# One buffer for an MLP chunk's activations and their sums, one copy and one subtraction to split it, and dependent sums spread over turns

## The chip, the cores and the metric

The kernel runs on one core of a Trainium2 chip. The metric is the time of one execution on the device in microseconds (us). Engines in the profile: PE is TensorE (PEld its weight loads), DVE is VectorE, ACT is ScalarE, POOL is GpSimd, SP is the engine whose queue issues most DMAs.

## The reference

One layer of a decoder trunk on 256 tokens of width 1024, in float32: a gated sum of a convolution branch and a sparse attention branch, a cross attention, and an MLP with squared relu, then a last RMSNorm. The change is in the MLP, and in a few buffers of the attention's index scores:

```python
def reference(x, mem, ...):
    ...
        h = h + (g_conv * y_conv + g_attn * y_attn) @ w_mix_out[l]
        h = h + _cross_attention(...)
        hf = _rmsnorm(h, norm_ffn_g[l]) @ w_ff1[l]            # (256, 1024) @ (1024, 4096)
        h = h + jnp.square(jax.nn.relu(hf)) @ w_ff2[l]        # (256, 4096) @ (4096, 1024)
    return _rmsnorm(h, norm_final_g)
```

## The kernel before

**Products in three terms.** The matmuls run in a rounded float32 format (`F32R`). To keep float32 accuracy both operands are split into a high part (a copy into `F32R`, on ScalarE) and a low part (the operand minus its high part, on VectorE), and a product is high*high + high*low + low*high (`mm3`). So each weight and each activation costs one ScalarE copy and one VectorE subtraction.

**The stream of weights.** All weights come in chunks of 1 MB (`raw`, 128 x 2048 elements) in the order of `STREAM`, through three buffers. `load()` issues the next one on SP's queue. It is called where the last low part of an earlier chunk is issued, so a load waits on the chip until that buffer's last reader, a VectorE subtraction, is done. Every chunk becomes a few jobs in `high_jobs` (normally two halves). `split_high()` takes the first job and issues its ScalarE copy; `split_low()` issues the VectorE subtraction of the job before it, and calls `prepare()` of the job that is second in the list; `split_ahead()` does one `split_low` and one `split_high`, and is called once per tile of matmuls. At most five halves are split ahead.

**The MLP.** The hidden width of 4096 is cut into 16 chunks of 256 features. `("f1", c)` is the slice of the first weight and `("f2", c)` that of the second. `first(x, side, wide)` computes 128 of the 256 features for all tokens into a PSUM bank `ps_f`, taken from the two `mm` banks. With `wide` the three terms go into two halves of a bank that have to be merged (a ScalarE copy and a VectorE sum). The loop over `c` does `first(c+2, 0)`, the first half of chunk c's second product, `first(c+2, 1)`, and its second half. So an activation is made two chunks ahead of its use.

**Chunks with seven products.** For the chunks in `SEVEN` the second product is a 2 x 2 block product of activation blocks (feature half k, token block r, each 128 x 128) and weight blocks (128 x 512). It is computed with seven block products instead of eight, which needs sums of blocks on both sides. The weight's sums (`seven`) are `outer` (two sums in one instruction) and `inner` (two instructions, of which the second reads the first's result); its jobs are `left`, `last`, `outer`, `inner`. The activation's sums (`fn`) are one instruction of two blocks and two instructions that depend on each other. Chunks 0, 1 and 5 use six products, chunks 13 to 15 four.

**The activation of a chunk** is a generator, `activation`, one for each 128 features (`ct`): relu out of PSUM and square on ScalarE into `ft`, the sums `fn` on VectorE, then for each group of blocks a ScalarE copy into `sh` and a VectorE subtraction into `sl` (both parts of `fs`). For a chunk with seven products these are three copies (1, 2 and 4 blocks) and three subtractions.

**Turns.** Generators are in `chains`. `tick()` runs each of them up to its next `yield`; it is called after each tile. `finish(chain)` calls `tick()` until that chain has ended, and `Hidden.done()` does so for both chains of a chunk. A turn thus advances all chains: besides the activations, `turn_rows` (sixteen small DMAs into `h_rm`, one in each turn) and `ff_scale`, which sums the squares of h (`sums_ff`) for the MLP's RMSNorm and, three turns after its last square, sends `ps_ff` matmuls to TensorE. The order in which the instructions are issued in this program is the order in which each engine runs them.

Of the kernel before, what the change touches and what calls it, by code (L numbers as in the profile page):

```python
# [114 lines left out]
def block_kernel(ctx, tc, x, xt, mem, memt, wst, wki, vecs, convw, gout, out):  # L115
# [21 lines left out]
    def w2(name, dt=F32, shape=(P, 512)):  # L137
        return work.tile(list(shape), dt, tag="w2", bufs=8, name=name)

    def bank(tag, bufs, name):  # L140
        return psum.tile([P, 512], F32, tag=tag, bufs=bufs, name=name)

# [58 lines left out]

    class Stage:

        def __init__(self, key, high, before=None, slot=True):
            self.key, self.high, self.before, self.slot = key, high, before, slot
            if not slot:
                elsewhere.add(key)

        def prepare(self):
            if self.before:  # L210
                self.before()
                self.before = None

    def seven(key, c, raw):

        b = raw.rearrange("p (k h n) -> p k h n", k=2, h=2)
        flat = raw.rearrange("p (j n) -> p j n", j=4)
        sums = []

        def outer():  # L220
            sums.append(t8(f"sums{c}", F32, (P, 4, 512)))
            dve.tensor_tensor(out=sums[0][:, 0:2, :], in0=flat[:, 0:4:3, :],
                              in1=flat[:, 1:2, :].to_broadcast([P, 2, 512]), op=ALU.add)

        def inner():
            t = sums[0]
            dve.tensor_tensor(out=t[:, 2, :], in0=t[:, 1, :], in1=flat[:, 0, :], op=ALU.add)
            dve.tensor_tensor(out=t[:, 3, :], in0=t[:, 2, :], in1=flat[:, 2, :], op=ALU.add)

        def stage(name, src_of, n, before=None):  # L230
            def high():
                src = src_of()
                if before:
                    both = t8(f"{name}{c}", F32R, (P, 2, 2, 512))
                    hi, lo = both[:, 0], both[:, 1]
                else:
                    hi = highs.tile([P, N_CHUNK // 2], F32R, tag="hi", name=f"hi{c}{name}")
                    lo = lows.tile([P, N_CHUNK // 2], F32R, tag="lo", name=f"lo{c}{name}")
                    hi, lo = (w[:, : n * 512].rearrange("p (j n) -> p j n", j=n) for w in (hi, lo))
                act(hi, src, AF.Copy)  # L240

                def low():
                    dve.tensor_tensor(out=lo, in0=src, in1=hi.bitcast(F32), op=ALU.subtract)
                    prepared[(*key, name)] = (hi, lo)
                    if name == "inner":
                        load()

                low_jobs.append(low)

            return Stage((*key, name), high, before, not before)  # L250

        return [stage("left", lambda: b[:, :, 0, :], 2), stage("last", lambda: flat[:, 3:4, :], 1),
                stage("outer", lambda: sums[0][:, 0:2, :], 2, outer), stage("inner", lambda: sums[0][:, 2:4, :], 2, inner)]

    def high(key, c, raw, ns, q, last):
        n = ns.stop - ns.start
# [16 lines left out]
    def split_high():  # L273
        if high_jobs and (not high_jobs[0].slot or nsplit[0] - nused[0] < HALVES - held[0]):
            job = high_jobs.pop(0)
            nsplit[0] += job.slot
            job.prepare()
            job.high()

    def split_low():  # L280
        if low_jobs:
            low_jobs.pop(0)()
        if len(high_jobs) > 1:
            high_jobs[1].prepare()

    nsplit, nused, held = [0], [0], [1]

# [149 lines left out]
    load()  # L437
    zero = w2("zero")
    nc.vector.memset(zero, 0.0)
    zero_r = cst.tile([P, 512], F32R, name="zero_r")  # L440
    nc.vector.tensor_copy(zero_r, zero)
    ident = cst.tile([P, P], F32, name="ident")
    make_identity(nc, ident)
# [3 lines left out]
    nc.gpsimd.memset(onesd, 1.0 / D)  # L447
    table = cst.tile([P, 1], F32, name="table")
    nc.gpsimd.memset(table, 0.0)
    ki2 = cst.tile([P, S], F32, name="ki2")  # L450

    nc.scalar.activation(half, half, AF.Sigmoid, bias=0.0, scale=0.0)
    nc.gpsimd.memset(half, -0.5)
# [185 lines left out]
    tick()  # L639
    wi = cst.tile([P, 2, 8], F32, name="wi")  # L640

    bias = [cst.tile([P, P * (qb + 1)], F32, name=f"bias{qb}") for qb in range(2)]

    def causal(t, qb, value):
        tail = t[:, qb * P :]
# [19 lines left out]
    def index_scores():  # L665
# [3 lines left out]
        dve.tensor_copy(wi, ps[:, :16].rearrange("p (r h) -> p r h", r=2))  # L669
        for qb in range(2):  # L670
            nk = P * (qb + 1)
            score = cst.tile([P, nk], F32, name=f"score{qb}")
            per = 512 // nk
            for g in range(4 // per):
                banks = [ps_acc(f"ps_idx{qb}{g}{j}").rearrange("p (a n) -> p a n", a=per) for j in range(2)]
                for a in range(per):
                    for j in range(2):
                        rows = slice(64 * j, 64 * j + 64)
                        pe.matmul(banks[j][:, a, :], qi_t[rows, per * g + a, qb * P : qb * P + P], ki2[rows, :nk],
                                  start=True, stop=True)  # L680
                for j in range(2):
                    rl = w2(f"rl{qb}{g}{j}", F32, (P, per, nk))
                    act(rl, banks[j], AF.Relu)
                    yield
                    for a in range(per):
                        h = 2 * (per * g + a) + j
                        if h == 0:
                            dve.tensor_scalar(score, rl[:, a, :], wi[:, qb, 0:1], None, ALU.mult)
                        else:
                            dve.scalar_tensor_tensor(out=score, in0=rl[:, a, :], scalar=wi[:, qb, h : h + 1], in1=score,  # L690
                                                     op0=ALU.mult, op1=ALU.add)
            causal(score, qb, NEG_FILL)
            yield
            fill.insert(0, choose(qb, score))
# [466 lines left out]
    start(turn_rows())  # L1161
    start(ff_scale())

    def activation(c, ct, ps, t, sh, sl):
        if ps.shape[1] == S:
            act(t[:, ct, :], ps, AF.Relu)  # L1166
        else:
            yield from merge(t[:, ct, :], ps)
            yield
            act(t[:, ct, :], t[:, ct, :], AF.Relu)  # L1170
        act(t[:, ct, :], t[:, ct, :], AF.Square)
        yield
        flat = t.rearrange("p k (r n) -> p (k r) n", r=2)
        if c not in SEVEN:
            cs = [(slice(2 * ct, 2 * ct + 2), flat[:, 2 * ct : 2 * ct + 2, :])]
        else:
            cs = [(slice(1, 3), flat[:, 2:4, :]) if ct else (slice(0, 1), flat[:, 0:1, :])]
        if ct and c < JOINED:
            n = w2(f"fn{c}", F32, (P, 4, P))
            if c in SEVEN:  # L1180
                dve.tensor_tensor(out=n[:, 0:2, :], in0=flat[:, 1:2, :].to_broadcast([P, 2, P]), in1=flat[:, 0:4:3, :],
                                  op=ALU.subtract)
                dve.tensor_tensor(out=n[:, 2, :], in0=flat[:, 0, :], in1=n[:, 1, :], op=ALU.subtract)
                dve.tensor_tensor(out=n[:, 3, :], in0=flat[:, 2, :], in1=n[:, 2, :], op=ALU.subtract)
                cs.append((slice(3, 7), n))
            else:
                dve.tensor_tensor(out=n[:, 0:2, :], in0=flat[:, 0:4:2, :], in1=flat[:, 1:4:2, :], op=ALU.subtract)
                cs.append((slice(4, 6), n[:, 0:2, :]))
        for js, src in cs:
            act(sh[:, js, :], src, AF.Copy)  # L1190
        yield
        for js, src in cs:
            dve.tensor_tensor(out=sl[:, js, :], in0=src, in1=sh[:, js, :].bitcast(F32), op=ALU.subtract)

    class Hidden:

        def __init__(self, c):
            self.c, self.jobs = c, []
            parts = t8(f"fs{c}", F32R, (P, 2, 7, P))
            self.hi, self.lo = parts[:, 0], parts[:, 1]  # L1200
            self.t = w2(f"ft{c}", F32, (P, 2, S))

        def after(self, ct, ps):
            self.jobs.append(start(activation(self.c, ct % 2, ps, self.t, self.hi, self.lo)))
# [2 lines left out]
            return self.hi[:, j, :], self.lo[:, j, :]  # L1207

        def row(self, k, rb):
            return self.of(2 * k + rb)  # L1210

        def done(self):
            for job in self.jobs:
# [31 lines left out]
            seventh(x, name)  # L1245
            tick()

    TERMS = {"left": (("1", 0), ("2", 1)), "last": (("3", 6),), "outer": (("5", 4), ("7", 3)), "inner": (("6", 5), ("4", 2))}

    def seventh(x, name):  # L1250
        w = weights("f2", x.c, name, None)
# [18 lines left out]
        return ap.rearrange("p (k f) -> p k f", f=P)  # L1270

    def last_residual(rb, ps, lo, hi):
        h = h_rm[:, lo // P : hi // P, rb, :]
        ps = by_tiles(ps)
        dve.scalar_tensor_tensor(out=h, in0=ps, scalar=r2[0][:, rb : rb + 1], in1=h, op0=ALU.mult, op1=ALU.add)

    def last_squares(rb, n, lo, hi):

        h = h_rm[:, lo // P : hi // P, rb, :]
        junk = w2(f"junk_o{rb}{n}")  # L1280
        act(by_tiles(junk[:, : hi - lo]), h, AF.Square, scale=1.0 / 32, accum_out=ss[:, rb, n : n + 1])
        if hi == D:
# [4 lines left out]
    def last_norm(rb, n):  # L1287
# [4 lines left out]
        for n, (lo, hi) in enumerate(((0, 352), (352, 704), (704, D))):  # L1292
# [2 lines left out]
                dve.tensor_scalar(cols, cols, scale, None, ALU.mult)  # L1295
            else:
                act(cols, cols, AF.Copy, scale=scale)
            (nc.scalar if n == 2 else nc.sync).dma_start(out[rb, :, lo:hi], cols)

    def add_to(rb, hf, ps, scales):  # L1300
        h = h_rm[:, 4 * hf : 4 * hf + 4, rb, :]
        dve.scalar_tensor_tensor(out=h, in0=by_tiles(ps), scalar=scales[:, rb : rb + 1], in1=h, op0=ALU.mult, op1=ALU.add)

    for c in range(JOINED):
        hidden.append(Hidden(c + 2))
        x, later = hidden[c], hidden[c + 2]
        wide = c not in SEVEN and c != 5
        first(later, 0, wide)
        x.done()
        if c in (0, 1, JOINED - 1):  # L1310
            split_ahead()
        half_of(x, 0)
# [130 lines left out]
```

## Time and profile before

| | |
|---|---|
| median of 3 runs | 505.08 us (504.98 to 505.32) |
| the profiled execution | 505.25 us, span 503.5 us |
| granted TensorE clock, mean | 0.998 |
| PE busy | 493.6 us, 98% of the span |
| DVE busy | 459.9 us, 91% |
| ACT busy | 349.1 us, 69% |
| POOL busy | 31.6 us, 6% |
| HBM read | 91.16 MB, 183 GB/s over the span |

The page gives shares over the whole span. A row of the timeline is: start in us from the span's start, duration in us, engine, line, operation, output <- inputs, partitions x elements, count, and in brackets the idle time of the engine before it and what ended that. Rows with a count above 1 are several instructions of one kind in sequence. A row of the chain that ended last has start, duration, engine and tile. Numbers of `ps_p`, `hi` and `lo` tiles are left out, but `hi58left` is the high part of the `left` job of `raw` number 58, which is `("f2", 2)`; 60, 62 and 66 are chunks 3, 4 and 6, and 74 is chunk 10. Most VectorE and TensorE operations go through one helper and so have the same line, L80. In the MLP stage the hidden chunk number 0 begins at about 323 us, and the last products end at about 497 us.

### The profile page before, as it was taken

Reading aid. Unit: us, or ns where it says so; the run is one execution under the profiler, and the core shown is the slowest. Engines: PE = TensorE matmul, PEld = TensorE weight load, DVE = VectorE, ACT = ScalarE, POOL = GpSimd, SP = SyncE. Lnnn points to the kernel's source line nnn. Section 1 sums busy time; section 2 is a strip of 40 time slices with the busy share of each in tenths; the row PEclk is TensorE's granted clock in tenths of the full one; section 3 lists DMA queues with packets and bytes.
Section 4 is the critical chain, followed back from the end, with each engine's and each line's share of the span. In section 5 each row is a group of like instructions: output and inputs, shape, how many; then the busy total and the mean of one; then the engine's idle time right before and its main releaser. Section 6 shows DMA issues by size and latency. Waiting matters only on the chain.

```text
span 503.5 us, 8292 instructions
## 1 busy us (share of the span) xinstructions
PE 493.6 (98%) x3119; PEld 444.1 (88%) x3119; DVE 459.9 (91%) x858; ACT 349.1 (69%) x639; POOL 31.6 (6%) x49
## 2 busy tenths in 40 slices
PE   7999999999999999999999999999999999999995
PEld 5999998888888888888889999988989899988984
DVE  5999999999999799999988986888999899999994
ACT  7657777788656676668756667586777677777832
POOL 2002212221021100000000000000000000000000
PEclk9999999999999999999999999999999999999999
DMA  8949678899787744345645454368855645544602
GB/s 312 381 184 280 185 191 261 226 246 262 225 265 215 191 148 144 119 158 197 246 169 218 175 174 161 127 192 214 239 181 184 235 159 206 221 178 168 251 1 84
DMA packets 27225, 100.36 MB, mean 199 GB/s; under 512 B 10656, under 2 KB 11552, under 8 KB 17200
## 3 DMA queue, kind: packets, MB, share of 16 engines
q1 hardware_dynamic: 23120, 92.90, 53.4%
q0 software_dynamic: 3632, 6.59, 7.3%
q8 instruction: 24, 0.39, 0.3%
q10 hardware_dynamic: 432, 0.33, 0.2%
q14 instruction: 17, 0.14, 0.1%
HBM read 91.16 MB, written 1.05 MB: 183 GB/s over the span
## 4 chain that ended last, share of the span: by engine, by line
PE 62%; DVE 18%; ACT 7%; DMA 7%; issue 5%; POOLq 0%; POOL 0%; DVEq 0%; ACTq 0%
PE ps_conv L80 10%; DMA raw<-in_wst_dram 6%; PE ps_f L80 6%; DVE lo L80 5%; PE ps_ao L80 4%; PE ps_q L80 4%; PE ps_k L80 4%; PE ps_ga L80 4%; PE ps_gc L80 4%; PE ps_v L80 4%; PE ps_xo L80 3%; DVE sums L80 3%; PE ps_qi L80 2%; PE ps_xk L80 2%; PE ps_p L80 2%
## 5 line engine op out<-in xcount | busy, mean ns | idle before, releaser
L80 DVE TENSOR_TENSOR lo<-raw,hi 128x1024 fp32r<-128x1024 f32 x141 | 170.5, 1214 | 5.2 <-ACT hi L263 5.1
L263 ACT ACTIVATE hi<-raw 128x1024 fp32r<-128x1024 f32 x141 | 146.7, 1046 | 2.0 <-DMA raw<-in_wst_dram 2.0
L80 PE MATMUL ps_f<-ff_p,hi 128*128 128x256 f32 (+1 forms) x448 | 92.8, 299 | 0.6 <-ACT ft L1166 0.3
L80 DVE SCALAR_TENSOR_TENSOR acc<-u,cw,acc 128x234 f32<-128x234 f32 (+29 forms) x190 | 78.0, 461 | 0.3
L80 PEld LDWEIGHTS ps_f<-ff_p,hi 128*128 128x128 f32 x448 | 72.8, 191 | 5.8 <-ACT ft L1166 2.0
L80 PE MATMUL ps_f<-ff_p,lo 128*128 128x256 f32 x256 | 70.9, 282 | 0.0
L80 PEld LDWEIGHTS ps_f<-ff_p,lo 128*128 128x128 f32 x256 | 48.8, 191 | 0.6
L80 PE MATMUL ps_conv<-n_p,hi 128*128 128x256 f32 x224 | 41.0, 285 | 0.0
L80 PEld LDWEIGHTS ps_conv<-n_p,hi 128*128 128x128 f32 x224 | 34.9, 192 | 0.8 <-issue 0.7
L80 PE MATMUL ps_conv<-n_p,lo 128*128 128x256 f32 x112 | 31.7, 283 | 0.0
L588 POOL DMA_DIRECT2D acc<-products x25 | 21.6, 864 | 125.1 <-ACT products L587 50.1
L80 PE MATMUL ps_p<-hi,fs 128*128 128x512 f32 (+1 forms) x88 | 27.2, 372 | 0.0
L80 PE MATMUL ps_q<-n_p,hi 128*128 128x512 f32 x64 | 23.6, 406 | 0.0
L80 PE MATMUL ps_k<-n_p,hi 128*128 128x512 f32 x64 | 23.5, 407 | 0.0
L80 PE MATMUL ps_ao<-o_p,hi 128*128 128x512 f32 x64 | 22.6, 401 | 0.0
L80 PE MATMUL ps_co<-u_p,hi 128*128 128x512 f32 (+1 forms) x80 | 22.2, 351 | 0.0
L80 PE MATMUL ps_mix<-mix_p,hi 128*128 128x512 f32 (+1 forms) x80 | 22.2, 351 | 0.0
L80 PE MATMUL ps_ga<-n_p,hi 128*128 128x512 f32 x64 | 22.0, 396 | 0.0
L80 PE MATMUL ps_gc<-n_p,hi 128*128 128x512 f32 x64 | 22.0, 396 | 0.0
L587 ACT ACTIVATE products<-u,cw 128x231 f32<-128x231 f32 (+24 forms) x50 | 21.9, 489 | 0.0
L80 PEld LDWEIGHTS ps_conv<-n_p,lo 128*128 128x128 f32 x112 | 21.5, 192 | 0.0
L80 PE MATMUL ps_v<-hi,n_p 128*128 128x512 f32 x64 | 19.9, 389 | 0.0
(386 smaller groups left out, 1215.8 us busy)
## 6 DMA issues: line engine op xcount, KB each, us to landing
raw<-in_wst_dram SPq DMA_DIRECT2D x76, 1024.0 KB, 4.9
acc<-products POOLq DMA_DIRECT2D x25, 256.0 KB, 5.3
raw<-in_wst_dram SPq DMA_DIRECT2D x12, 512.0 KB, 7.6
x_rm<-in_x_dram SPq DMA_DIRECT2D x2, 512.0 KB, 4.2
mem_rm<-in_mem_dram SPq DMA_DIRECT2D x1, 1024.0 KB, 8.9
mem_t<-in_memt_dram SPq DMA_DIRECT2D x1, 1024.0 KB, 10.9
h_t<-in_xt_dram SPq DMA_DIRECT2D x1, 1024.0 KB, 7.0
h_rm<-turned SPq DMA_DIRECT2D x16, 64.0 KB, 5.6
```

Source lines behind the costliest of these rows:

```text
L80: return fn(*args, **kwargs)
L263: act(hi, raw[:, ns], AF.Copy)
L587: act(prod[:, a, s:], u[:, t, : S - s], AF.Copy, scale=cw[:, t, TAPS - 1 - s : TAPS - s])
L588: nc.gpsimd.dma_start(acc[:, ts, :], prod, accum_op=ALU.add)
```

## The change

- The activation of a chunk, its sums and all its parts are laid out in one buffer of eight blocks, `ft` of a new tag `w4` with two buffers (before: `ft` and `fn`, of the tag `w2` with eight). Relu is still done per 128 features; for `ct == 0` the generator then ends. The square is taken once for all four blocks. The sums go into the blocks behind them, each in a turn of its own where it depends on another. Then comes one copy and one subtraction for all parts (7, 6 or 4 blocks). Chunk 15 keeps doing it by halves.
- The sums are ordered so that the needed blocks are contiguous; for that the two token blocks change places in the numbering (`1 - rb`, `TERMS`).
- The sums of the weights become `steps`. Each `split_low` runs one step of the first job that has one among the first three of the list. `inner` has two steps.
- `x.done()` is called ahead of `first(later, 0, wide)`, not behind it.
- `zero_r`, `ki2`, `bias` and `score` move from their own places into the two buffers of `w4`.

The core of the diff:

```diff
+    def w4(name, dt=F32, shape=(P, KT, P)):
+        return work.tile(list(shape), dt, tag="w4", bufs=2, name=name)
...
-        def prepare(self):
-            if self.before:
-                self.before()
-                self.before = None
+        def step(self):
+            self.steps.pop(0)()
...
-        def inner():
+        def inner(j):
             t = sums[0]
-            dve.tensor_tensor(out=t[:, 2, :], in0=t[:, 1, :], in1=flat[:, 0, :], op=ALU.add)
-            dve.tensor_tensor(out=t[:, 3, :], in0=t[:, 2, :], in1=flat[:, 2, :], op=ALU.add)
+            dve.tensor_tensor(out=t[:, j, :], in0=t[:, j - 1, :], in1=flat[:, 2 * j - 4, :], op=ALU.add)
...
+                stage("outer", lambda: sums[0][:, 0:2, :], 2, (outer,)),
+                stage("inner", lambda: sums[0][:, 2:4, :], 2, (lambda: inner(2), lambda: inner(3)))]
...
     def split_low():
         if low_jobs:
             low_jobs.pop(0)()
-        if len(high_jobs) > 1:
-            high_jobs[1].prepare()
+        for job in high_jobs[:3]:
+            if job.steps:
+                job.step()
+                break
...
-    zero_r = cst.tile([P, 512], F32R, name="zero_r")
+    zero_r = w4("zero_r", F32R, (P, 512))
...
-    ki2 = cst.tile([P, S], F32, name="ki2")
+    picked = w4("picked", F32, (P, D))
+    ki2 = picked[:, 3 * S :]
...
+    def relu(ps, t):
+        if ps.shape[1] == S:
+            act(t, ps, AF.Relu)
+        else:
+            yield from merge(t, ps)
+            yield
+            act(t, t, AF.Relu)
+
+    def part(c, t, js, sh, sl):
+        act(sh[:, js, :], t, AF.Copy)
+        yield
+        dve.tensor_tensor(out=sl[:, js, :], in0=t, in1=sh[:, js, :].bitcast(F32), op=ALU.subtract)
...
     def activation(c, ct, ps, t, sh, sl):
+        if c == 15:
+            yield from by_halves(c, ct, ps, t, sh, sl)
+            return
+        yield from relu(ps, t[:, 2 * ct : 2 * ct + 2, :].rearrange("p r n -> p (r n)"))
+        if ct == 0:
+            return
+        act(t[:, 0:4, :], t[:, 0:4, :], AF.Square)
+        yield
+        js = slice(0, 4)
+        if c in SEVEN:
+            dve.tensor_tensor(out=t[:, 4:6, :], in0=t[:, 0:1, :].to_broadcast([P, 2, P]), in1=t[:, 1:3, :], op=ALU.subtract)
             yield
+            dve.tensor_tensor(out=t[:, 6, :], in0=t[:, 1, :], in1=t[:, 5, :], op=ALU.subtract)
+            yield
+            dve.tensor_tensor(out=t[:, 7, :], in0=t[:, 3, :], in1=t[:, 6, :], op=ALU.subtract)
+            yield
+            js = slice(1, 8)
+        elif c < JOINED:
+            dve.tensor_tensor(out=t[:, 4:6, :], in0=t[:, 1:4:2, :], in1=t[:, 0:4:2, :], op=ALU.subtract)
+            yield
+            js = slice(0, 6)
+        yield from part(c, t[:, js, :], slice(0, js.stop - js.start), sh, sl)
...
-            self.t = w2(f"ft{c}", F32, (P, 2, S))
+            self.t = w4(f"ft{c}")
...
         wide = c not in SEVEN and c != 5
+        x.done()
         first(later, 0, wide)
-        x.done()
         if c in (0, 1, JOINED - 1):
             split_ahead()
         half_of(x, 0)
```

More of the change, by code (lines that the diff above doesn't have):

```diff
@@ L202, in block_kernel, with __init__ @@
     class Stage:
-        def __init__(self, key, high, before=None, slot=True):
-            self.key, self.high, self.before, self.slot = key, high, before, slot
+        def __init__(self, key, high, steps=(), slot=True):
+            self.key, self.high, self.steps, self.slot = key, high, list(steps), slot
             if not slot:
                 elsewhere.add(key)
-        def prepare(self):
-            if self.before:
-                self.before()
-                self.before = None
+        def step(self):
+            self.steps.pop(0)()
     def seven(key, c, raw):
@@ L223, in outer, with stage @@
                               in1=flat[:, 1:2, :].to_broadcast([P, 2, 512]), op=ALU.add)
-        def inner():
+        def inner(j):
             t = sums[0]
-            dve.tensor_tensor(out=t[:, 2, :], in0=t[:, 1, :], in1=flat[:, 0, :], op=ALU.add)
-            dve.tensor_tensor(out=t[:, 3, :], in0=t[:, 2, :], in1=flat[:, 2, :], op=ALU.add)
-        def stage(name, src_of, n, before=None):
+            dve.tensor_tensor(out=t[:, j, :], in0=t[:, j - 1, :], in1=flat[:, 2 * j - 4, :], op=ALU.add)
+        def stage(name, src_of, n, steps=()):
             def high():
                 src = src_of()
-                if before:
+                if steps:
                     both = t8(f"{name}{c}", F32R, (P, 2, 2, 512))
@@ L248, in high @@
                 low_jobs.append(low)
-            return Stage((*key, name), high, before, not before)
+            return Stage((*key, name), high, steps, not steps)
         return [stage("left", lambda: b[:, :, 0, :], 2), stage("last", lambda: flat[:, 3:4, :], 1),
-                stage("outer", lambda: sums[0][:, 0:2, :], 2, outer), stage("inner", lambda: sums[0][:, 2:4, :], 2, inner)]
+                stage("outer", lambda: sums[0][:, 0:2, :], 2, (outer,)),
+                stage("inner", lambda: sums[0][:, 2:4, :], 2, (lambda: inner(2), lambda: inner(3)))]
     def high(key, c, raw, ns, q, last):
@@ L276, in split_high @@
             nsplit[0] += job.slot
-            job.prepare()
+            while job.steps:
+                job.step()
             job.high()
@@ L282, in split_low @@
             low_jobs.pop(0)()
-        if len(high_jobs) > 1:
-            high_jobs[1].prepare()
+        for job in high_jobs[:3]:
+            if job.steps:
+                job.step()
+                break
     nsplit, nused, held = [0], [0], [1]
@@ L640, in block_kernel @@
     wi = cst.tile([P, 2, 8], F32, name="wi")
-    bias = [cst.tile([P, P * (qb + 1)], F32, name=f"bias{qb}") for qb in range(2)]
+    bias = [picked[:, :P], picked[:, P : 3 * P]]
     def causal(t, qb, value):
@@ L671, in index_scores @@
             nk = P * (qb + 1)
-            score = cst.tile([P, nk], F32, name=f"score{qb}")
+            score = picked[:, (3 + qb) * P : (3 + qb) * P + nk]
             per = 512 // nk
@@ L1162, in block_kernel @@
     start(ff_scale())
-    def activation(c, ct, ps, t, sh, sl):
[L1165 to L1168, printed above, removed]
-            yield
[L1170 to L1193, printed above, removed]
@@ new lines, in relu, with by_halves @@
+    def relu(ps, t):
[9 more added lines that the diff above has]
+        dve.tensor_tensor(out=sl[:, js, :], in0=t, in1=sh[:, js, :].bitcast(F32), op=ALU.subtract)
+    def by_halves(c, ct, ps, t, sh, sl):
+        js = slice(2 * ct, 2 * ct + 2)
+        yield from relu(ps, t[:, js, :].rearrange("p r n -> p (r n)"))
+        act(t[:, js, :], t[:, js, :], AF.Square)
+        yield
+        yield from part(c, t[:, js, :], js, sh, sl)
@@ new lines, in activation @@
+    def activation(c, ct, ps, t, sh, sl):
+        if c == 15:
[9 more added lines that the diff above has]
+            dve.tensor_tensor(out=t[:, 4:6, :], in0=t[:, 0:1, :].to_broadcast([P, 2, P]), in1=t[:, 1:3, :], op=ALU.subtract)
+            yield
+            dve.tensor_tensor(out=t[:, 6, :], in0=t[:, 1, :], in1=t[:, 5, :], op=ALU.subtract)
[5 more added lines that the diff above has]
+            dve.tensor_tensor(out=t[:, 4:6, :], in0=t[:, 1:4:2, :], in1=t[:, 0:4:2, :], op=ALU.subtract)
+            yield
+            js = slice(0, 6)
+        yield from part(c, t[:, js, :], slice(0, js.stop - js.start), sh, sl)
@@ L1209, in row @@
         def row(self, k, rb):
-            return self.of(2 * k + rb)
+            return self.of(2 * k + 1 - rb)
         def done(self):
@@ L1246, in half_of @@
             tick()
-    TERMS = {"left": (("1", 0), ("2", 1)), "last": (("3", 6),), "outer": (("5", 4), ("7", 3)), "inner": (("6", 5), ("4", 2))}
+    TERMS = {"left": (("1", 0), ("2", 2)), "last": (("3", 6),), "outer": (("5", 4), ("7", 3)), "inner": (("6", 5), ("4", 1))}
     def seventh(x, name):
@@ L1272, in last_residual @@
     def last_residual(rb, ps, lo, hi):
-        h = h_rm[:, lo // P : hi // P, rb, :]
+        h = h_rm[:, lo // P : hi // P, 1 - rb, :]
         ps = by_tiles(ps)
-        dve.scalar_tensor_tensor(out=h, in0=ps, scalar=r2[0][:, rb : rb + 1], in1=h, op0=ALU.mult, op1=ALU.add)
+        dve.scalar_tensor_tensor(out=h, in0=ps, scalar=r2[0][:, 1 - rb : 2 - rb], in1=h, op0=ALU.mult, op1=ALU.add)
     def last_squares(rb, n, lo, hi):
-        h = h_rm[:, lo // P : hi // P, rb, :]
+        h = h_rm[:, lo // P : hi // P, 1 - rb, :]
         junk = w2(f"junk_o{rb}{n}")
@@ L1297, in last_norm @@
                 act(cols, cols, AF.Copy, scale=scale)
-            (nc.scalar if n == 2 else nc.sync).dma_start(out[rb, :, lo:hi], cols)
+            (nc.scalar if n == 2 else nc.sync).dma_start(out[1 - rb, :, lo:hi], cols)
     def add_to(rb, hf, ps, scales):
-        h = h_rm[:, 4 * hf : 4 * hf + 4, rb, :]
-        dve.scalar_tensor_tensor(out=h, in0=by_tiles(ps), scalar=scales[:, rb : rb + 1], in1=h, op0=ALU.mult, op1=ALU.add)
+        h = h_rm[:, 4 * hf : 4 * hf + 4, 1 - rb, :]
+        dve.scalar_tensor_tensor(out=h, in0=by_tiles(ps), scalar=scales[:, 1 - rb : 2 - rb], in1=h, op0=ALU.mult, op1=ALU.add)
     for c in range(JOINED):
```

## The prediction

> **What bounds the kernel now.** I read the page's busy line, the busy time by stage, TensorE's instructions in order of time, and then the chain that ended last.
>
> ```profile
> PE 493.6 (98%) x3119; PEld 444.1 (88%) x3119; DVE 459.9 (91%) x858; ACT 349.1 (69%) x639; POOL 31.6 (6%) x49
> ```
>
> ```profile
> 425.00:450.00 25.00, 25.00 (x166) 22.88 (x165) 24.70 (x34) 18.64 (x32) 0.00 (x0) 1.00 0.55 210
> ```
>
> In the MLP stage (323 us to 497 us) TensorE and VectorE are both nearly full. A busy TensorE may be a waiting one, so I looked at the distance between the starts of its matmuls: 0.12 us for 256 columns and 0.23 us for 512. In this stage it widens in three places only:
>
> ```profile
> 371.88 0.39 PE L80 MATMUL ps_p<-hi60last,fs 128*128 128x512 f32 x1
> 372.56 0.50 PE L80 MATMUL ps_f<-ff_p,hi 128*128 128x256 f32 x2 [0.29 <-ACT ft L1166]
> ...
> 394.24 0.39 PE L80 MATMUL ps_p<-hi,fs 128*128 128x512 f32 x1
> 394.76 0.51 PE L80 MATMUL ps_f<-ff_p,hi 128*128 128x256 f32 x2
> ...
> 458.03 0.39 PE L80 MATMUL ps_p<-hi76last,fs 128*128 128x512 f32 x1
> 458.55 0.50 PE L80 MATMUL ps_f<-ff_p,hi 128*128 128x256 f32 x2
> ```
>
> The starts lie 0.68, 0.52 and 0.52 apart instead of 0.23, and the next pair takes 0.1 more each time: 1.3 us lost in all. That is the most that a lighter VectorE can return. Each time a `ps_f` tile waits for a relu (`ft`) to empty its bank: the sum "7" holds one of the two `mm` banks to the end, so from its first product on only one is left. The relu stands in ScalarE's queue behind weight copies that wait for VectorE's sums or for a load. What sets those is a loop over the three `raw` buffers, which the chain shows:
>
> ```profile
> 346.18 5.38 DMA raw<-in_wst_dram
> 351.58 1.07 ACT hi58left L240
> 352.67 1.23 DVE lo58left L80
> ...
> 357.37 6.24 DMA raw<-in_wst_dram
> 363.63 1.07 ACT hi60left L240
> ...
> 380.19 4.82 DMA raw<-in_wst_dram
> 385.03 1.07 ACT hi L263
> ...
> 388.51 4.84 DMA raw<-in_wst_dram
> 393.38 1.06 ACT hi66left L240
> ```
>
> A load starts when the last low part of the chunk three loads earlier has been taken; the high and low parts of the chunk that landed follow; among the work behind them is the low part that starts the next load of this kind. Up to 394.76 TensorE has no lead left over it: whatever lengthens this loop up to 393.38 moves TensorE's wait at 394.76 by as much.
>
> **The change part by part.** *VectorE's work for a seven-product chunk.* One chunk in the steady stretch:
>
> ```profile
> 439.48 0.28 DVE L80 TENSOR_TENSOR fs<-ft,fs 128x128 fp32r<-128x128 f32 x1
> 439.76 1.22 DVE L80 TENSOR_TENSOR lo74left<-raw,hi74left 128x1024 fp32r<-128x1024 f32 x1
> 440.90 0.69 DVE L80 TENSOR_TENSOR lo74last<-raw,hi74last 128x512 fp32r<-128x512 f32 x1
> 441.50 1.22 DVE L80 TENSOR_TENSOR sums<-raw 128x1024 f32<-128x1024 f32 x1
> 442.64 0.42 DVE L80 TENSOR_TENSOR fn<-ft 128x256 f32<-128x256 f32 x1
> 443.09 0.62 DVE L80 TENSOR_TENSOR fn<-ft,fn 128x128 f32<-128x128 f32 x2
> 443.63 1.22 DVE L80 TENSOR_TENSOR lo<-raw,hi 128x1024 fp32r<-128x1024 f32 x1
> 444.76 1.41 DVE L80 TENSOR_TENSOR sums<-sums,raw 128x512 f32<-128x512 f32 x2
> 446.09 0.42 DVE L80 TENSOR_TENSOR fs<-ft,fs 128x256 fp32r<-128x256 f32 x1
> 446.42 0.68 DVE L80 TENSOR_TENSOR fs<-fn,fs 128x512 fp32r<-128x512 f32 x1
> 447.02 1.22 DVE L80 TENSOR_TENSOR outer<-sums,outer 128x1024 fp32r<-128x1024 f32 x1
> ...
> 450.43 0.28 DVE L80 TENSOR_TENSOR fs<-ft,fs 128x128 fp32r<-128x128 f32 x1
> ```
>
> From `fs` to `fs` a chunk takes 10.95 (439.48 to 450.43); TensorE's matmuls for it take 48 x 0.12 + 21 x 0.23 = 10.6. From start to start the three subtractions take 0.28 + 0.33 + 0.60 = 1.21; one over 896 elements, between the 512 (0.60) and the 1024 (1.14), takes about 1.0: 0.2 less. The dependent `fn` sums take 0.45 + 0.54; apart they would take 0.34 + 2 x 0.2: 0.25 less. The dependent pair of `sums` takes 1.33, apart 1.2: 0.13 less. Together 0.58, so VectorE needs 10.4 and is no longer behind TensorE by its work alone.
>
> The Trainium skill ("VectorE: DVE Perf Modes", The DRAIN you can't avoid) says that every op drains in any case and that a semaphore between two of them costs nothing extra. By that, spreading dependent sums returns nothing, VectorE stays at 10.75 and the faster outcome below would end at 504.2 instead of 503.8. The dependent pair (1.33 against 1.2) does not agree with it.
>
> *ScalarE* loses one square and two of three copies a chunk. It has slack (18.64 of 25): nothing by itself.
>
> *The loop.* What counts is the order in which VectorE gets its work between a landing and the f1 low part that starts the next such load. Before: left, last, outer `sums`, `fn`, f1. After: left, outer `sums` (one call earlier), last, the first inner sum, activation steps, f1. In the steady stretch that is 1.14 + 1.13 + 0.60 + 0.60 + 0.34 = 3.81 against 443.63 - 439.76 = 3.87: no change. In the first stretch it costs, because the chunks made in `wide` tiles have two more turns for their merge, and their one big subtraction falls between left and f1:
> - after `hi58left` starts: 1.09 to the low part, 1.13 left, 1.13 outer, 0.22 last sum of chunk 2's activation, 0.60 last, 0.60 inner, 1.0 subtraction of chunk 2, 0.34 merge of chunk 3, 1.22 f1, 0.05 to the issue: 7.4. Today 357.37 - 351.58 = 5.8, chunk 2's subtractions being done by then in idle time: +1.6.
> - after `hi60left`: 1.1 + 1.13 + 1.13 + 0.60 + 0.60 + 1.0 (chunk 3) + 0.34 + 1.22 + 0.05 = 7.2. Today the next such load landed at 374.58, took 4.8, and so began 6.2 after 363.63: +1.0.
> - after `hi62left`: 1.16 + 1.13 + 1.13 + 0.60 + 0.60 + 0.34 + 1.25 = 6.2 against 380.19 - 374.58 = 5.6: +0.6.
> - from 385.03 to 388.51 no step is moved: 0.
>
> ```profile
> 374.58 1.06 ACT L240 ACTIVATE hi62left<-raw 128x1024 fp32r<-128x1024 f32 x1 [0.37 <-DMA raw<-in_wst_dram]
> ```
>
> *The moved `x.done()`.* For every chunk after the first the activation has ended by then. Chunk 0 has three turns to go, and until now the two turns inside the wide `first` covered what was left. Now three turns run ahead of `first(2, 0)`, with everything that the other chains have due in them: the fold of `sums_ff`, the `ps_ff` matmuls, chunk 1's steps, three issues of `h_rm` on SP (they wait for nothing but `turned`, done by then, and hold up no load).
>
> ```profile
> 332.84 0.62 ACT L896 ACTIVATE sq_ff<-h_t 128x512 f32<-128x512 f32 x1
> ...
> 334.10 0.42 ACT L1171 ACTIVATE ft<-ft 128x256 f32<-128x256 f32 x1
> ...
> 334.69 1.05 ACT L263 ACTIVATE hi<-raw 128x1024 fp32r<-128x1024 f32 x1
> ```
>
> ```profile
> 332.88 0.42 DVE L80 TENSOR_TENSOR ft<-ps_f,ft 128x256 f32<-128x256 f32 x1
> 333.22 1.21 DVE L80 TENSOR_TENSOR lo<-raw,hi 128x1024 fp32r<-128x1024 f32 x1
> ```
>
> ```profile
> 333.78 0.63 PE L80 MATMUL ps_f<-ff_p,hi 128*128 128x512 f32 x2
> ...
> 338.16 0.50 PE L80 MATMUL ps_ff<-onesd,sums_ff 128*128 128x2 f32 x4
> 338.52 0.49 PE L80 MATMUL ps_p<-hi,fs 128*128 128x512 f32 x1
> ```
>
> ```profile
> 334.46 0.34 SPq L176 DMA_DIRECT2D raw<-in_wst_dram  x1
> ```
>
> ```profile
> 340.25 1.06 ACT L263 ACTIVATE hi<-raw 128x1024 fp32r<-128x1024 f32 x1 [0.59 <-DMA raw<-in_wst_dram]
> ```
>
> On ScalarE `sq_ff` comes 0.42 earlier (a square less ahead of it) and ends at 333.05; relu and double square follow to 334.0, chunk 1's merge copy to 334.4. VectorE: merge until 333.3, the two folding sums until 334.4 (0.69 and 0.42), chunk 0's difference until 334.7, a merge until 335.0. ScalarE: the copy of 768 elements (0.84, between 0.62 and 1.05) until 335.6, chunk 1's relu and double square until 336.55. VectorE: chunk 0's subtraction until 336.55, chunk 1's difference until 337.0.
>
> So on TensorE the tile of 333.78 stands behind `ps_ff`, which waits for the fold until 334.4 and takes 0.36 (338.16 to 338.52) that is saved there: 0.6 late, which the later waits absorb. On VectorE the low part of 333.22 starts at 337.0. It starts a load (334.46) that ScalarE waits for at 340.25: it goes out 3.7 later, at 338.2, and with 4.8 to 5.75 to its landing the copy runs at 343.1 to 344.0. From there to the end of the low part that starts the load of 346.18 come copy 0.95, relu 0.3, copy 0.95, merge copy 0.35, merge 0.4, low part 1.2: that load begins at 347.3 to 348.3. +1.1 to +2.1; I take +1.6, as neither landing is nearer.
>
> The landings of 346.18 (5.38) and 357.37 (6.24) are longer than the others (4.8); small `h_rm` transfers ran beside them, which now go out earlier. 0 to 0.55 and 0 to 1.4 less; no row tells how much, so the middle, -0.3 and -0.7.
>
> *At no cost:* `zero_r`, `ki2`, `bias` and `score` in one buffer keep their regions apart and their order of use (if whole tiles waited for each other, the index matmuls would wait for VectorE's scores); swapped parts and `1 - rb` rows change no count; `sums` takes its slot one call earlier, where nothing waits for a slot today.
>
> **Sum.** At 394.76: 1.6 - 0.3 + 1.6 - 0.7 + 1.0 + 0.6 = +3.8 (ends +2.3 and +5.3). After that the order is the steady one, and ScalarE's inner copy waits for one sum after f1 and not two, so the wait of 458.55 (0.4) goes: +3.4. The profiled execution took 505.25 and the median of the runs is 505.08; against the median 508.5, ends 507.0 and 510.0.
>
> **The rivals.** *Faster:* VectorE's work and not the loop is what binds; the three waits go, the late start is absorbed: 505.08 - 1.3 = 503.8. VectorE at 24.70 of 25 speaks for it; against it, ScalarE waits for landings (0.59, 0.37) with VectorE's next part queued behind. It decides if the load of 346.18 starts no later and the big subtractions meet idle time. The Trainium skill ("Perfetto Trace Analysis", Identifying the Most-Contended Engine) says to optimize the engine with the highest occupancy first, which is this case. *About the same:* the late load at the start is hidden and both long landings shrink to 4.8: -0.55 + 1.6 - 1.4 + 1.0 + 0.6 - 0.4 = +0.85, 505.9. For it: the ScalarE copy at 351.58 has room if other work is as late anyway; against it, the order of the code, in which that load hangs on the moved part.
>
> **Numbers.** Slower by the loop 0.70, own range 507.0 to 510.0; whole-tile waits 0.02, beyond 510; about the same 0.15; faster 0.13. Less than 0.2% (1.0 us) can't be told from none. The range takes in the case at 505.9 and reaches halfway from there to the faster one, and 0.6 over the upper end for durations estimated between rows: 504.5 to 510.6.
>
> **What would show it.** The `ps_ff` matmuls ahead of chunk 2's first tile behind a gap of 0.6; the loads of 334.46 and 346.18 at about 338 and 348; one `fs` subtraction of about 1.08; waits of a few us on TensorE up to 394 and none at 458. If the load of 346.18 is not later, the start was wrong; if it is and TensorE does not wait, the loop was.

## The result, and the profile after

| | before | after |
|---|---|---|
| median | 505.17 us (504.56 to 506.57, 6 runs) | 508.74 us (508.22 to 510.87, 6 runs) |
| profiled execution | 505.25 us, span 503.5 us | 508.37 us, span 506.6 us |
| granted TensorE clock, mean | 0.998 | 0.996 |

The ratio is 1.0077, 95% interval [1.0054, 1.01]: the change makes the kernel about 0.8% slower.

The page's busy line after:

```profile
PE 494.9 (98%) x3119; PEld 444.8 (88%) x3119; DVE 455.8 (90%) x830; ACT 343.2 (68%) x596; POOL 31.7 (6%) x49
```

VectorE has 28 instructions and 4.1 us of work less, ScalarE 43 and 5.9 us less, and the kernel takes 3.1 us more. The busy time by stage, in the same stretch as before, shows both lighter too (24.05 and 16.68 against 24.70 and 18.64). Its columns are the stretch and its length, then busy us and instructions of PE, PEld, DVE, ACT and POOL, the granted clock, the DMA share and GB/s:

```profile
425.00:450.00 25.00, 25.00 (x168) 23.09 (x167) 24.05 (x31) 16.68 (x23) 0.00 (x0) 1.00 0.47 174
```

So the change did what it says, and the loss is elsewhere. TensorE's instructions in order of time after:

```profile
333.95 0.40 PE L80 MATMUL ps_f<-ff_p,hi 128*128 128x512 f32 x1
334.75 0.61 PE L80 MATMUL ps_ff<-onesd,sums_ff 128*128 128x2 f32 x4 [0.41 <-DVE sums_ff L80]
...
366.72 1.52 PE L80 MATMUL ps_p<-inner,fs 128*128 128x512 f32 x6
368.39 0.50 PE L80 MATMUL ps_f<-ff_p,hi 128*128 128x256 f32 x2
...
374.79 0.51 PE L80 MATMUL ps_f<-ff_p,hi 128*128 128x256 f32 x2 [1.21 <-ACT ft L1171]
...
385.23 0.39 PE L80 MATMUL ps_p<-hi62last,fs 128*128 128x512 f32 x1
385.73 0.50 PE L80 MATMUL ps_f<-ff_p,hi 128*128 128x256 f32 x2
...
398.10 0.50 PE L80 MATMUL ps_f<-ff_p,hi 128*128 128x256 f32 x2 [0.87 <-ACT ft L1171]
```

The tile that began at 394.76 begins at 398.10. The row at 366.72 holds six matmuls that start 0.23 apart, so the tile of 368.39 comes 0.3 late. By distances between starts, TensorE loses 4.2 us in the MLP stage (1.4 before, the 1.3 of the prediction and 0.1 behind the `ps_ff` matmuls). All but 0.2 us of it lies ahead of 398.5, and nothing is left at 458.

The chain that ended last shows the circle of loads:

```profile
338.54 5.43 DMA raw<-in_wst_dram
343.99 1.06 ACT hi L264
...
348.23 5.09 DMA raw<-in_wst_dram
353.34 1.07 ACT hi58left L240
...
360.73 4.89 DMA raw<-in_wst_dram
365.64 1.07 ACT hi60left L240
...
372.80 4.75 DMA raw<-in_wst_dram
377.58 1.07 ACT hi62left L240
...
383.74 4.70 DMA raw<-in_wst_dram
388.46 1.07 ACT hi L264
...
391.94 4.75 DMA raw<-in_wst_dram
396.72 1.07 ACT hi66left L240
```

The load that went out at 334.46 goes out at 338.54, that of 346.18 at 348.23, and `hi66left` follows at 396.72, where it stood at 393.38. What holds up the first of them is VectorE's order behind `x.done()`:

```profile
335.95 0.96 DVE L80 TENSOR_TENSOR fs<-ft,fs 128x768 fp32r<-128x768 f32 x1 [0.19 <-ACT fs L1178]
336.92 0.43 DVE L80 TENSOR_TENSOR ft<-ft 128x256 f32<-128x256 f32 x1
337.26 1.22 DVE L80 TENSOR_TENSOR lo<-raw,hi 128x1024 fp32r<-128x1024 f32 x1
```

That low part stood at 333.22 before. On the leg behind `hi58left` (the stretch from the start of that copy to the next load) the order is left, outer sums, last sum of the activation, last, first inner sum, the big subtraction, merge, f1:

```profile
354.43 1.23 DVE L80 TENSOR_TENSOR lo58left<-raw,hi58left 128x1024 fp32r<-128x1024 f32 x1 [3.00 <-ACT hi58left L240]
...
357.51 0.69 DVE L80 TENSOR_TENSOR sums<-sums,raw 128x512 f32<-128x512 f32 x1
358.12 1.09 DVE L80 TENSOR_TENSOR fs<-ft,fs 128x896 fp32r<-128x896 f32 x1
359.12 0.42 DVE L80 TENSOR_TENSOR ft<-ps_f,ft 128x256 f32<-128x256 f32 x1
359.45 1.22 DVE L80 TENSOR_TENSOR lo<-raw,hi 128x1024 fp32r<-128x1024 f32 x1
```

VectorE waited 3.00 us for `hi58left` just before: this work is in the way not because VectorE is full, but because it stands on the wrong side of a landing.

### The profile page after: what moved, and what is told of

It reads as the page before. It is cut to its first block, busy times and chain, and to the rows that moved or that the text cites. A ratio compares the mean times of both kernels' runs of the same rounds, so it can differ in the third digit from the quotient of the medians.

```text
span 506.6 us, 8228 instructions
## 1 busy us (share of the span) xinstructions
PE 494.9 (98%) x3119; PEld 444.8 (88%) x3119; DVE 455.8 (90%) x830; ACT 343.2 (68%) x596; POOL 31.7 (6%) x49
## 4 chain that ended last, share of the span: by engine, by line
PE 56%; DVE 18%; DMA 12%; ACT 7%; issue 5%; POOLq 0%; POOL 0%; DVEq 0%; ACTq 0%; SPq 0%
DMA raw<-in_wst_dram 12%; PE ps_conv L80 9%; DVE lo L80 4%; PE ps_ao L80 4%; PE ps_q L80 4%; PE ps_k L80 4%; PE ps_ga L80 4%; PE ps_gc L80 4%; PE ps_v L80 4%; DVE sums L80 4%; PE ps_xo L80 3%; ACT hi L264 2%; PE ps_qi L80 2%; PE ps_xk L80 2%; PE ps_xv L80 2%
## 5 line engine op out<-in xcount | busy, mean ns | idle before, releaser
L240 ACT ACTIVATE inner<-sums 128x1024 fp32r<-128x1024 f32 x10 | 10.6, 1061 | 16.1 <-DVE sums L80 16.1
```

## The experiments

Two theories. *The circle of loads*: the time is set by when loads go out through three buffers, so what counts is what stands on VectorE between a landing and the low part that frees a buffer. *The rival*: TensorE is late because of VectorE's work or order as such, and late loads are a symptom. All ratios below are to the kernel before, measured on the same chip in the same series. The changed kernel itself was measured in the first series alone, so differences to it go across series; the medians of the kernel before in them are 505.17 to 505.43 us.

**One part alone: the moved `x.done()`** in the kernel before.

```diff
-        first(later, 0, wide)
         x.done()
+        first(later, 0, wide)
```

> The kernel before, with x.done() ahead of first(later, 0, wide) and nothing else. Loop theory (the loss comes through the circle of loads over three raw buffers): VectorE's low part of 333.22 starts about 3 later, behind two turns of activation work; the load of 334.46 goes out at about 337.4 and that of 346.18 at about 348.0; the landings of that load and the next shorten by about 1.1 since fewer h_rm transfers stand beside them; TensorE's wait at 394.76 ends 0.7 later: 505.9 (505.2 to 506.7) against 505.2. Rival (the loss is in TensorE's wait for ps_ff and in longer single instructions that hold up the relus in ScalarE's queue): the move alone puts no ps_ff ahead and changes no instruction's size: 505.2.

Measured 506.96 us (506.37 to 508.96), ratio 1.0036 [1.0022, 1.0051]. One call moved by one place costs about half of the whole loss by the medians, and somewhat over a third by the profiled executions (506.42 and 505.25). It is more than the 505.9 (505.2 to 506.7) of the loop theory. SP's queue shows the load at the predicted time, and VectorE what stands ahead of its low part:

```profile
337.42 0.34 SPq L176 DMA_DIRECT2D raw<-in_wst_dram  x1
...
347.81 0.33 SPq L176 DMA_DIRECT2D raw<-in_wst_dram  x1
```

```profile
335.81 0.42 DVE L80 TENSOR_TENSOR fs<-fn,fs 128x256 fp32r<-128x256 f32 x1
336.14 1.22 DVE L80 TENSOR_TENSOR lo<-raw,hi 128x1024 fp32r<-128x1024 f32 x1
```

Of the 1.6 us at 346.18, 1.1 arrive at TensorE's meeting point (395.87 against 394.76), where 0.7 was expected. The rival, which gave the move alone no cost, falls.

**One part undone: the sums of chunks 2 and 3 in one turn**, so that their big subtraction comes ahead of the left part.

```diff
-            yield
+            if c > 3:
+                yield
```
(at each of the three yields between the sums)

> The changed kernel, with the three sums and the copy of chunks 2 and 3 in one turn (the yields between them only from chunk 4 on), so that their 896-element subtractions come before the left parts and not between left and f1. Loop theory: the way from hi58left to the next load shortens from 7.4 to 6.2, and from hi60left from 7.2 to 6.2; TensorE's wait that ends at 398.1 ends 2.2 earlier: 506.5 against 508.7. Rival (instruction sizes and ScalarE's queue): the same instructions, dependent sums again back to back: 508.7 or a little more.

Measured 507.57 us (506.81 to 508.43), ratio 1.0039 [1.0025, 1.0052], between the two expectations. The profiled execution is the slowest of its runs, and its chain shows both the gain and where it went there:

```profile
353.73 1.07 ACT hi58left L240
...
359.91 6.19 DMA raw<-in_wst_dram
366.12 1.07 ACT hi60left L240
372.28 4.71 DMA raw<-in_wst_dram
```

The legs shrink from 7.39 to 6.18 and from 7.16 to 6.16 as the order of work says; then the landing takes 6.19 us instead of 4.89 and `hi60left` starts no earlier than after the change. The legs are shown by this, the size of the gain is not.

**One part undone: the weights' sums issued as before.**

```diff
-        for job in high_jobs[:3]:
-            if job.steps:
-                job.step()
-                break
+        if len(high_jobs) > 1:
+            while high_jobs[1].steps:
+                high_jobs[1].step()
```

> The changed kernel, with the sums of the weights issued as before (all steps of the second job in the list at once: outer behind last, both inner sums behind f1). Loop theory: 0.6 leaves each of the three ways from a left part to the next load (7.4, 7.2 and 6.2 become 6.8, 6.6 and 5.6), TensorE's wait at 398.1 ends 1.8 earlier: 506.9. Rival (ScalarE's queue holds up the relus): the inner copy waits for two sums again, 0.7 later at each of the waits at 374 and 385: 509.4.

Measured 507.3 us (506.66 to 507.85), ratio 1.0036 [1.0026, 1.0047]. TensorE's rows at the two meeting points:

```profile
374.37 0.50 PE L80 MATMUL ps_f<-ff_p,hi 128*128 128x256 f32 x2 [1.20 <-ACT ft L1170]
...
396.62 0.50 PE L80 MATMUL ps_f<-ff_p,hi 128*128 128x256 f32 x2 [0.20 <-ACT ft L1170]
```

396.62 instead of 398.10: 1.5 earlier, where the loop theory had 1.8. The early order of the weights' sums, with an inner sum ahead of the f1 low part, costs about 1.4 us, though the sums take no more time on VectorE than before. The rival's 509.4 falls.

**Both undone**, the moved `x.done()` and the single copy and subtraction kept (the two edits above together).

> The changed kernel with both of the later legs put back: chunks 2 and 3 make their sums in one turn (so their 896-element subtraction comes before the left part), and the weights' sums are issued as in the kernel before. The moved x.done() and the one big copy and subtraction stay. Loop theory: the legs from hi58left, hi60left and hi62left to their next loads become 5.6 to 5.8, 5.6 to 6.2 and 5.6 to 5.8 (7.39, 7.16 and 6.16 in the changed kernel), the late load of 346.18 (at 348.2) stays; TensorE's wait at 398 goes: like the kernel before with the move alone, 506.0 to 506.9. Rival (landing times that vary set the stretch, and the gains of the two single experiments, 1.2 and 1.4 us, do not add): 507.3 to 507.6.

Measured 506.0 us (505.2 to 506.7), ratio 1.0009 [0.9996, 1.0022]. The gains add (1.2 and 1.4 singly, 2.7 together), so the rival falls. The chain:

```profile
348.06 5.04 DMA raw<-in_wst_dram
353.12 1.07 ACT hi58left L240
...
358.71 6.45 DMA raw<-in_wst_dram
```

The leg is 5.59, the start as late as after the change. The time is also 1.0 under that of the kernel before with the move alone (506.96): TensorE's wait at 373 is 0.74 here and 1.59 there. Why it is shorter was not taken apart.

**`x.done()` put back behind the tile**, the rest of the change kept (this needs three buffers of `w4` and six of `w2`).

```diff
-        x.done()
         first(later, 0, wide)
+        x.done()
```

> The changed kernel with x.done() behind first(later, 0, wide) as before; for that the tag w4 has three buffers and w2 six. Loop theory: the load of 348.23 goes out about 2 earlier, the landing after next gets 0 to 0.7 longer again beside h_rm transfers; the rest of the lag (the big subtractions and the early inner sum) stays: 506.9 (506.5 to 507.4). Rival (TensorE's wait for ps_ff and instruction sizes): only the 0.6 at ps_ff comes back: 508.1.

Measured 508.16 us (507.82 to 508.82), ratio 1.0053 [1.0038, 1.0067]. The number is the rival's and the reason is neither's. The load goes out early (334.29), as expected. But now chunk 0's one copy and one subtraction are issued only after the tile, and the products that need them are next on TensorE:

```profile
336.66 0.50 PE L80 MATMUL ps_ff<-onesd,sums_ff 128*128 128x2 f32 x4
338.09 0.51 PE L80 MATMUL ps_p<-hi,fs 128*128 128x512 f32 x1 [0.93 <-ACT fs L1178]
338.43 0.39 PE L80 MATMUL ps_p<-lo,fs 128*128 128x512 f32 x1
339.08 0.73 PE L80 MATMUL ps_p<-hi,fs 128*128 128x512 f32 x2 [0.26 <-DVE fs L80]
```

In the kernel before, where three small copies and subtractions make these parts, the products at 338.52 follow without a wait. So the merged split and the moved call belong together: without the move TensorE waits for the split, with it the load is late. What the waiting brought on besides in the profiled execution, the longest of the six, stands in the last section.

**The start mended another way**: as the kernel with both undone, and ahead of chunk 2's first tile only chunk 0's own chain is advanced, by two turns (its sum and its copy).

```diff
-        x.done()
+        if c:
+            x.done()
+        else:
+            for _ in range(2):
+                next(x.jobs[1])
         first(later, 0, wide)
+        x.done()
```

> As a_two, and x.done() ahead of chunk 2's first tile is replaced for chunk 0 alone: only its own chain is advanced by two turns there (its sum and its copy), then the tile follows, and the rest of done() behind it; so the low part that starts the load stands ahead of the fold of sums_ff, of chunk 0's 768-element subtraction and of chunk 1's steps. Loop theory: that low part starts at about 334.4 (before 333.22, changed 337.26), its load at 335.6 (334.46, 338.54), the load of 346.18 no later than 346.9 (348.23 in the changed kernel), chunk 0's subtraction ends by 337.4 in time for the products at 337.7, so TensorE does not wait there; no wait over 0.6 us up to 398: 504.6 to 505.4. Rival (the start is hidden behind the legs, or TensorE waits for chunk 0 as with x.done() put back): as a_two or worse, 506 to 508.

Measured 504.71 us (504.44 to 506.93), ratio 0.9996 [0.9985, 1.0008]: the whole loss is gone with the single copy, the single subtraction, the one buffer and the new numbering of the blocks still in. VectorE's rows have the low part at 334.53 (334.4 expected):

```profile
334.53 1.22 DVE L80 TENSOR_TENSOR lo<-raw,hi 128x1024 fp32r<-128x1024 f32 x1
...
336.73 0.95 DVE L80 TENSOR_TENSOR fs<-ft,fs 128x768 fp32r<-128x768 f32 x1
```

The two loads go out at 335.81 and 347.25 (335.6 and no later than 346.9 expected). One step missed: the subtraction ends at 337.68, TensorE asks for it at 337.15 and loses 0.59. No other wait of TensorE in the stage is over 0.1.

**A fourth buffer for loads**, the order of work untouched: first in the changed kernel, then in the one before.

```diff
-    raws = ctx.enter_context(tc.tile_pool(name="raws", bufs=3))
+    raws = ctx.enter_context(tc.tile_pool(name="raws", bufs=4))
...
-        return work.tile(list(shape), dt, tag="w2", bufs=8, name=name)
+        return work.tile(list(shape), dt, tag="w2", bufs=4, name=name)
...
+    load()
     hidden = [Hidden(0), Hidden(1)]
```
(five buffers of `w2` in the kernel before)

> The changed kernel with four raw buffers in place of three (two of them paid for by work buffers of 2 KB) and one load more issued before the MLP, so four loads are under way; order of work on all engines as in the changed kernel. Loop theory: a load is then issued a whole chunk earlier than its landing is needed, ScalarE's weight copies no longer wait for DMA between 338 and 397 us (in the changed kernel 4.21 us at 343.99 and the six landings of the chain after it), TensorE's waits at 374.79 (1.36) and 398.10 (1.03) go and only the 0.57 behind the ps_ff matmuls stays: 508.5 - 3.8 + 0.6 = about 505.0, range 504.2 to 505.8. Rival (VectorE's work in this stretch is what makes TensorE late, the loads only look late because they are issued behind it): the order is unchanged, so the waits stay and the time is 508 to 509.

Measured 504.53 us (504.4 to 505.2), ratio 0.9983 [0.9974, 0.9992]: 4.2 us off the changed kernel. Rows of ScalarE's left copies:

```profile
350.05 1.06 ACT L240 ACTIVATE hi58left<-raw 128x1024 fp32r<-128x1024 f32 x1 [0.55 <-DMA raw<-in_wst_dram]
361.50 1.05 ACT L240 ACTIVATE hi60left<-raw 128x1024 fp32r<-128x1024 f32 x1
372.91 1.04 ACT L240 ACTIVATE hi62left<-raw 128x1024 fp32r<-128x1024 f32 x1
389.19 1.04 ACT L240 ACTIVATE hi66left<-raw 128x1024 fp32r<-128x1024 f32 x1
```

`hi66left` at 389.19 instead of 396.72, and of TensorE's waits only that ahead of `ps_ff` stays (0.58). One copy, `hi58left`, still waits 0.55 for its landing, but no wait of TensorE comes of it. The order of work on TensorE, VectorE and ScalarE, which the rival blames, is the changed kernel's to the instruction.

> The kernel before with four raw buffers and one load more issued before the MLP. Loop theory: the copies at 340.25 (0.59) and 374.58 (0.37) no longer wait for a landing and with them TensorE's waits at 372.56 and 394.76 (0.9 together) go; the one at 458.55 (0.4) hangs on two dependent sums behind a low part and may stay: 504.2 to 504.6. Rival (VectorE's own work sets the waits): no difference, 505.2.

Measured 503.77 us (503.69 to 504.1), ratio 0.9972 [0.9961, 0.9982]: better than the 504.2 expected, since the wait at 458.55 goes as well. By distances between starts TensorE waits nowhere in the MLP stage but for the 0.1 behind `ps_ff`, and it is busy all through the stretch ahead of the meeting point (busy time by stage, the columns as before):

```profile
323.00:400.00 77.00, 77.00 (x464) 68.66 (x463) 72.07 (x112) 59.35 (x108) 0.00 (x0) 1.00 0.65 203
```

TensorE's 77.00 stood at 76.58 in the kernel before and 74.25 in the changed one, and VectorE does more here, 72.07 of 77, than in the kernel before (69.90) or after (64.22).

**Both ideas together**: the changed kernel with four buffers, and chunk 0's own chain advanced by three turns ahead of the tile; beside it the kernel before with four buffers again.

> The changed kernel with four raw buffers (a_raw4), and x.done() ahead of chunk 2's first tile replaced for chunk 0 alone: only its own chain is advanced, by three turns (sum, copy, subtraction), so the ps_ff matmuls go out behind that tile again. Loop theory: the last wait of a_raw4, 0.57 us ahead of ps_ff at 333.6, goes, and no other comes in its place: 503.8 to 504.0, the same as the kernel before with four buffers, since without a wait on TensorE the lighter VectorE and ScalarE have nothing to give. Rival (the lighter VectorE is worth something by itself once the circle of loads is gone): below 503.4, and faster than the kernel before with four buffers by more than 0.1 %.

> The kernel before with four raw buffers once more, on the same chip as a_raw4_own. Loop theory: 503.8 (503.77 the first time), within 0.1 % of a_raw4_own. Rival: slower than a_raw4_own by more than 0.1 %.

Measured 504.72 us (504.52 to 510.61), ratio 0.9987 [0.996, 1.0014], and 503.78 us (503.68 to 509.89), ratio 0.997 [0.9944, 0.9997]. The first missed: the wait did not go, it moved.

```profile
338.09 0.39 PE L80 MATMUL ps_p<-hi,fs 128*128 128x512 f32 x1
339.00 0.61 PE L80 MATMUL ps_ff<-onesd,sums_ff 128*128 128x2 f32 x4 [0.52 <-DVE sums_ff L80]
```

With `sums_ff`'s chain not advanced early, its fold now ends behind the tile, and `ps_ff` asks for it there: 0.68. So the two lie 0.19% apart, where under 0.1% was expected, and the slower one is the one with the lighter VectorE. In this series one run of each kernel lies some 6 us above its others, which widens the intervals. That a lighter VectorE gives something once the circle is gone is not seen in any run, but a changed kernel with no wait at all was not reached, so it is not excluded to the last tenth. The fastest version of all is the kernel before with a fourth buffer, 0.28% under the kernel before with three.

## Why the prediction was right

It forecast 508.5 us, and 508.74 was measured. Its terms against the trace of the changed kernel:

| step | predicted | measured |
|---|---|---|
| gap ahead of `ps_ff` | 0.6 | 0.57, and 0.08 behind it |
| low part of 333.22 | 337.0 | 337.26 |
| load of 334.46 | 338.2 | 338.54 |
| load of 346.18 later by | 1.6 (1.1 to 2.1) | 2.05 |
| its landing | -0.3 (0 to -0.55) | -0.29 |
| leg behind `hi58left` | 7.4, +1.6 | 7.39, +1.6 |
| its landing | -0.7 (0 to -1.4) | -1.35 |
| leg behind `hi60left` | 7.2, +1.0 | 7.16, +1.0 |
| leg behind `hi62left` | 6.2, +0.6 | 6.16, +0.6 |
| 385.03 to the next load | 0 | 0 (3.48 both) |
| sum at 394.76 | +3.8 | +3.34 |
| from there to the end | -0.4 | -0.2 |
| big subtraction, 896 elements | about 1.08 | 1.09 |

- *What bounds it* was right: a kernel whose TensorE is 98% and VectorE 91% busy was bound in this stretch by a circle of latencies. The four-buffer kernels show this; the single parts show where the change lengthened it.
- *The legs*, worked out from VectorE's order and rows of the profile before, came out to 0.05 us each; the measured terms add to 3.5, and the later landings took 0.2 less together. Of the two unknown landings one came out at the middle that was taken (-0.29 for -0.3), the other took nearly all of its range (-1.35 for -0.7); and the load of 346.18 went out 0.45 later than taken. These two errors cancel in part (+0.45, -0.65). The sum was good to 0.5 us because of that, and not because each term was: in that part it was luck.
- *Why a landing shrinks* is not shown. The prediction put the long landings down to `h_rm` transfers beside them, which would now go out earlier. The load of 360.73 did land in 4.89 us with almost no small packets beside it (16 under 512 bytes, against 1287 beside the load of 357.37 before). But with the sums in one turn the same load took 6.19 with 38 of them, and with both undone 6.45 with 46. So few small packets are not enough for a short landing.
- *VectorE's work* came out as well, and yet the time rose. From `lo74left` to `lo76left` a chunk takes it 10.93 us in the changed kernel (443.23 to 454.16), of which it stands idle for 0.48: 10.45 of work, 10.4 predicted. Its two weight sums, now apart, take 0.60 each as worked out.
- *The end*: the wait of 458.55 (0.39) went as predicted, and two distances at 476.48 grew by 0.1 each.
- Of the 3.1 us between the two profiled executions, TensorE's waits account for 2.8 (4.2 against 1.4) and a later start of the stage for 0.2 (its first tile at 323.0 and 322.8).
- *The faster rival* went by VectorE's load. Its condition was that the load of 346.18 start no later and that the big subtractions meet idle time; neither held. The page beside it in the Trainium skill ("Perfetto Trace Analysis", Identifying the Most-Contended Engine) pointed the same way: it judges TensorE by the share of its weight loads, among others, and that (88%) lies under VectorE's 91%. The trace disagrees: VectorE's work fell from 459.9 to 455.8 us and the time rose. The same page also says (Optimization Strategy) to find the gaps of the engine that one works on and what they wait for; in this trace that way leads to the loads (the 3.00 us of VectorE ahead of 354.43 end with the copy of a chunk that has just landed).
- *About the same*: of its two conditions the landings held in part (the second shrank by 1.35 of 1.4, the first by 0.29 of 0.55), the hidden start did not. The move alone shows 1.1 of it at TensorE.

## What to carry to other kernels

When every engine is nearly full, look at how far apart the starts of the bounding engine's instructions are, follow each widening back, and count what lies between a landing and the instruction that frees a buffer for the next load: an instruction that moves to the wrong side of that point costs its whole length, however cheap it has become. Here one call moved by one place cost 1.7 us, and 10 us less work on VectorE and ScalarE made no version clearly faster than the kernel before with as many buffers for loads. Before tuning the order of such a circle, try one buffer more, paid for by small ones that are not needed. Merging small steps into one big step made the engines' work less here, but the first result later; where a product waits for the first part, that is paid for.

## What the runs showed of the hardware

**TensorE's clock fell after waits of about 1.5 us in all.** In the kernel with `x.done()` put back, TensorE had little to do from 336.8 to 339.1 (the four rows above). The busy time by stage right behind it, and for comparison in the changed kernel:

```profile
340.00:343.00 3.00, 3.00 (x9) 2.35 (x8) 3.00 (x4) 2.89 (x4) 0.00 (x0) 0.51 0.40 117
```

```profile
340.00:343.00 3.00, 3.00 (x18) 2.57 (x17) 2.17 (x2) 0.00 (x0) 0.00 (x0) 1.00 0.79 314
```

Half the matmuls in the same time at a granted clock of 0.51. It is 0.50 from 340.1 to 343.5, which by the distances between starts (0.43 for 512 columns and not 0.23) costs some 1.6 us there, as much as the waits themselves. Less than half of that shows at the end: this execution has a mean granted clock of 0.994 and takes 508.82 us, the other five have 0.996 to 0.999, as those of the other kernels, and take 507.82 to 508.28. A fall of 3.4 us to one half takes 0.003 off the mean, and no execution of any kernel has more than 0.999, so at least the two at 0.998 and 0.999 (508.16 and 508.28) had none, and the fall is not the reason for the median. A single wait of 1.59 us (`x.done()` alone, at 373.66) and one of 1.36 (after, at 374.79) brought no such fall; the granted clock behind them is 1.00. (With `x.done()` alone two executions that were not profiled have 0.994 and 0.995, and they are its longest, 508.96 and 508.62; whether their clock fell in the same way is open.) The Trainium skill ("TensorE: Matmul & The Clock Gate", What's actually happening) says that the clock halves after at least one idle window of about 3.4 us that runs freely. Here there was no stretch of 3.4 us without matmuls, so the rule as stated doesn't give this; what sets the threshold wasn't tried.

**The same load takes 4.7 to 6.5 us to land**, and which one is slow changes from trace to trace (359.91 above with 6.19, 360.73 with 4.89, 358.71 with 6.45). With three buffers these landings are on the path, and the times lie 2.7 us apart in the changed kernel (508.22 to 510.87) and 4.1 in one series of the kernel before (504.21 to 508.35). With four buffers the kernel before lies within 0.4 us in its first series (503.69 to 504.1) and, but for the one execution at 509.89, in its second (503.68 to 504.08).
